# Byte margins for matmul operands, and an attention buffer that is shared with the scores

## The chip, the cores and the metric

The kernel runs on one core of a Trainium2 chip. The metric is the device time of one execution in microseconds (us), lower is better. The core has five engines that run their own instruction streams in order and wait for each other through semaphores: TensorE (PE, its weight loads listed apart as PEld), VectorE (DVE), ScalarE (ACT), GpSimd (POOL) and SyncE (SP, which here issues DMAs).

## The reference

One layer of an encoder over 512 tokens of width 1024. A combined projection of 11,328 columns feeds three branches: neighbourhood attention (16 heads of 64, a window of 8 by 16 on a grid 64 wide), a bidirectional Mamba-2 state-space mixer (8 groups, 32 heads), and two sigmoid gates that merge them. An output projection, two layer norms and a squared-ReLU feed-forward part (1024 to 4096 to 1024) follow.

```python
def hybrid_mixer(u, ...):
    proj = u @ w_in
    q, k, v, z, xbc, dt_raw, gate = jnp.split(proj, offs, axis=-1)
    ya = neighbourhood_attention(q, k, v, rpb) @ w_attn_br
    ...
    y = y * jax.nn.silu(z)            # y: the state-space scan, both directions
    ...
    ys = y @ w_ssd_br
    gates = jax.nn.sigmoid(gate + b_gate)
    merged = gates[:, :, 0] * ya + gates[:, :, 1] * ys
    return merged @ w_o

h = layer_norm(x, ln0_g, ln0_b)
h = layer_norm(ALPHA * h + hybrid_mixer(h, ...), ln1_g, ln1_b)
h = layer_norm(ALPHA * h + jnp.square(jax.nn.relu(h @ w1)) @ w2, ln2_g, ln2_b)
```

Within attention, for each head: scores are the scaled products of a query with the keys of its window plus a bias, softmax over the window, and the sum of values with these weights.

## The kernel before

All products are made in three: each fp32 operand is split into a high part and a low remainder (names ending in h and l, or wh and wl for weights), and `mm3` (lines 352 to 354) adds high times high, high times low and low times high in one PSUM bank. ScalarE makes the high part of a weight slab by a copy, and VectorE or GpSimd the low one by a subtraction. Slabs of weights have 8 blocks of 128 rows by 256 columns, 8 KB in each partition. Their high and low parts sit in two buffers each, of a pool named wp (tags wh and wl), which are reused through the whole kernel.

The stages, in order of time: first layer norm and transposes; eight groups of the state-space mixer, each with its projections (ps_x, and ps_z with the weights as the moving operand, 256 columns a product) beside the scan; attention; the attention branch's projection (ps_abr); the output projection (ps_o, 256 columns a product); the feed-forward part, whose first half product begins early in 256 columns; and the second feed-forward matrix, where the squared activations sq are the moving operand (ps_f from wh_f and sq). The mixer's order is made by a planner from costs; attention is written in plain order, and the framework's scheduler sets the order on each engine.

An operand of a product begins at some byte of its partition's memory. Which byte it is within 256 follows from the sizes of all tiles that stand ahead of it in the pools. Small unused tiles (rx_pad, ge_pad) set it here and there. As the tiles are laid out, in (moving operand, stationary operand): most 512-column products stand at (0, 0), those of wh_f with sq at (0, 128), z at (0, 0), group 0's x and the early feed-forward products at (0, 0), the output projection at (0, 96) and (192, 96), attention's scoring at (0, 64 or 128; 0), and the product of weights and values (po) at (128, 0).

Attention runs over 8 pairs of heads. For each head:

- TensorE makes two score banks pss (lines 1213 and 1214). VectorE adds the bias, writes the scores to sc and their maximum to mx (line 1218, a custom operation), and negates mx (1222).
- ScalarE takes the exponentials of the four quarters of sc in place and adds up sums (1224). VectorE inverts sums (reciprocal, 1226) and normalises sc (1228).
- TensorE transposes sc into two banks tp_p (1239). ScalarE copies each into pth (1243); VectorE subtracts for ptl (1244).
- TensorE makes po in ten products (1251 and 1252). Since the values' high and low parts stand side by side in the stationary operand vhl, one half of po's partitions holds the low part's sum. ScalarE copies it to low (1262), and VectorE adds both halves into aT (five additions, 1265).

sc has two buffers, so head h + 2 uses that of head h; low has a buffer of its own. Gate projections (ps_g, their sigmoid at line 1060) and the weights of later pairs are laid between heads by the scheduler. ScalarE loads a function table when it goes from the sigmoid to the exponential or back.

Of the kernel before, what the change touches and what calls it, by code (L numbers as in the profile page):

```python
# [11 lines left out]
F32 = mybir.dt.float32  # L12
F32R = mybir.dt.float32r
# [6 lines left out]
P = 128  # L20
# [3 lines left out]
KD = D // P  # L24
D_INNER = 2048
D_FF = 4096
NH = 16
HD = 64
# [5 lines left out]
OFF_Q, OFF_K, OFF_V, OFF_Z = 0, 1024, 2048, 3072  # L34
# [34 lines left out]
W0_ENG = lambda nc: (nc.gpsimd, nc.vector, nc.gpsimd, nc.vector)  # L69
# [3 lines left out]
class Plan:  # L73
# [16 lines left out]
                self.ap = self.make()  # L90
            return self.ap

    def tile(self, name, tag, pool, shape, dtype):
        return Plan.Tile(self, name, tag, lambda: pool.tile(shape, dtype, tag=tag, bufs=self.tags[tag],
                                                            name=name))

    def have(self, name, tag, ap):
        t = Plan.Tile(self, name, tag, None)
# [214 lines left out]
def encoder_layer(ctx, tc, x, w_in, w_attn_br, w_ssd_br, w_o, w_ff1, w_ff2, pcols, rows64,  # L313
                  d_skip, ln_rows, rpb_pad, consts, lmask, out, dbg=None):
    nc = tc.nc
# [6 lines left out]
    wp = ctx.enter_context(tc.tile_pool(name="wp", bufs=2))  # L322
# [20 lines left out]
                              op=ALU.subtract)  # L343
        return hi, lo

    def weights(parts, nk, ncol, name, eng=nc.vector, pool=None, after=None):
        hi = (pool or wp).tile([P, nk, ncol], F32R, tag="wh", name=f"wh_{name}")
        lo = (pool or wp).tile([P, nk, ncol], F32R, tag="wl", name=f"wl_{name}")
        return split_weights(parts, nk, ncol, name, hi, lo, eng, pool, after)

    def mm3(o, lh, ll, rh, rl, start, stop):
# [52 lines left out]
    gep = ge.__enter__()  # L404
# [33 lines left out]
    def by_dir(t, c, g):  # L438
# [13 lines left out]
    def local(name, tag, shape, dtype=F32):  # L452
        return plan.tile(name, tag, sbp, shape, dtype)

    def slab(name, parts, nk, ncol, engs):

        ws = plan.tile(f"ws_{name}", "ws", wp, [P, nk, ncol], F32)
        wh = plan.tile(f"wh_{name}", "wh", wp, [P, nk, ncol], F32R)
        wl = plan.tile(f"wl_{name}", "wl", wp, [P, nk, ncol], F32R)
        c = 0  # L460
        keys = []
        for j, (src, r0, c0, n) in enumerate(parts):
            op("SP", 4.0 * n / ncol, lambda src=src, r0=r0, c0=c0, n=n, c=c: nc.sync.dma_start(
                ws()[:, :, c : c + n],
                src[r0 : r0 + nk * P, c0 : c0 + n].rearrange("(k p) c -> p k c", p=P)),
               r=[("behind", 0)], w=[(ws.name, j)], at=4.8 if name == "x0" else 4.4)
            keys.append((ws.name, j))
            c += n
        hk = nk // 2
        for i, (k, eng) in enumerate(zip((slice(0, hk), slice(hk, nk)), engs)):  # L470
            op("ACT", 1.06, lambda k=k: nc.scalar.activation(wh()[:, k], ws()[:, k], AF.Copy),  # L471
               r=keys, w=[(wh.name, i)])
# [13 lines left out]
    def load_x(t):  # L486
# [7 lines left out]
       r=[(xts[0].name, 0)], w=[(xts[2].name, 0), ("behind", 0)])  # L494
# [11 lines left out]
    for t in range(NT):  # L506
        for j in range(2):
            op("DVE", 0.68, lambda t=t, j=j: v_.bn_stats(sts[t][:, j, :], xts[t]()[:, halves2[j]]),
               r=[(xts[t].name, 0)], w=[("st", t, j)])
        op("DVE", 0.2, lambda t=t: v_.bn_aggr(mv[:, t, :], sts[t]), r=[("st", t, 0), ("st", t, 1)],  # L510
           w=[("mv", t)])
    for ts in ((0,), (1,), (2, 3)):

        pr = slice(ts[0], ts[-1] + 1)
        vh, nv, y = lv[:, pr, 0], lv[:, pr, 1], rs[:, pr, 0]
        op("ACT", 0.28, lambda pr=pr, vh=vh: a_.activation(vh, mv[:, pr, 1], AF.Sqrt, bias=eps),
           r=[("mv", t) for t in ts], w=[("vh", ts[0])], table="sqrt")
# [12 lines left out]
    for t in range(NT):  # L530
# [19 lines left out]
       r=[(ws_dt.name, 0), (wh_dt.name, 0)], w=[(wl_dt.name, 0)], lock=True)  # L550
# [212 lines left out]

    def group_slabs(g):
        wb = slab(f"bc{g}", [(w_in, 0, OFF_B + g * P, P), (w_in, 0, OFF_C + g * P, P)], KD, 256,
                  (nc.gpsimd, nc.gpsimd) if g else W0_ENG(nc)[:2])
        wx = slab(f"x{g}", [(w_in, 0, OFF_X + g * 256, 256)], KD, 256,
                  (nc.gpsimd, nc.gpsimd) if g else W0_ENG(nc)[2:])
        return wb, wx

    def z_project(g):
        wh, wl = slab(f"z{g}", [(w_in, 0, OFF_Z + g * 256, 256)], KD, 256, (nc.gpsimd, nc.gpsimd))
        sz = local(f"sz{g}", "sz", [P, NT, 256])
        for c2 in range(2):
            ps = bank(f"ps_z{g}_{c2}", "mm", [P, 2, 256])
            for j in range(2):
                c = slice((2 * c2 + j) * P, (2 * c2 + j + 1) * P)
                for k in range(0, KD, 2):
                    def mms(k=k, j=j, c=c, ps=ps):
                        for q in (k, k + 1):  # L780
# [325 lines left out]
    vpool = tc.tile_pool(name="vp", bufs=1, reuse_waits="tile")  # L1106
    vpp = vpool.__enter__()

    vhl = vpp.tile([P, 4, NH // 2, 4, HD], F32R, name="vhl")

    hb = tc.tile_pool(name="hb", bufs=1, reuse_waits="tile")
    hbp = hb.__enter__()
# [43 lines left out]
    for pr in range(NH // 2):  # L1156
# [3 lines left out]

        qf = atp.tile([P, S], F32, tag="qf", name=f"qf{pr}")
        nc.scalar.activation(qf, psq, AF.Copy, scale=0.125)
        qs = atp.tile([P, 2, 4, 8, 16], F32R, tag="qs", name=f"qs{pr}")
        halves = (slice(0, HD), slice(HD, P))
        for hh, hp in enumerate(halves):
            for sv, dv in q_views(qf[hp], qs[hp, hh]):
# [15 lines left out]
        for hh in range(2):  # L1182
# [19 lines left out]
                    in1=cst[:, CC_M0 + half * P : CC_M0 + (half + 1) * P].rearrange(  # L1202
                        "p (r j) -> p r j", r=8), op=ALU.add)
            sc = atp.tile([P, 4, 256], F32, tag="sc", bufs=2, name=f"sc{h}")
            mx = atp.tile([P, 4], F32, tag="mx", bufs=2, name=f"mx{h}")
            sums = atp.tile([P, 4], F32, tag="sums", bufs=2, name=f"sums{h}")
            for m2 in range(2):
                pss = psx.tile([P, 2, 256], F32, tag="so", bufs=BANKS["so"], name=f"pss{h}_{m2}")
# [49 lines left out]
            pv(3, 0, 1, 3, False, False)  # L1258
            pv(3, 1, 1, 0, False, True)

            low = atp.tile([P, 4, P], F32, tag="low", name=f"low{h}")
            nc.scalar.activation(low[hp], po[HD - hh * HD : P - hh * HD], AF.Copy)
            pov, lov = (t[hp].rearrange("p m (r i) -> p m r i", r=8) for t in (po, low))
            for (dv, sv), (_, lv) in zip(q_views(aT[hp, pr, :], pov), q_views(aT[hp, pr, :], lov)):
# [30 lines left out]
    rx0 = tc.tile_pool(name="rx0", bufs=1, side="right", reuse_waits="tile")  # L1295
    rx0p = rx0.__enter__()
    rows0 = rx0p.tile([P, 2, D], F32, name="rows0")
    rx0p.tile([P, 8], F32, name="rx_pad")

    def first_norm(t, xt, eng):  # L1300

# [49 lines left out]
    w3p = ctx.enter_context(tc.tile_pool(name="w3", bufs=1, reuse_waits="tile"))  # L1351
    ep = tc.tile_pool(name="ep", bufs=1, reuse_waits="tile")
    epp = ep.__enter__()
    wo_pool = tc.tile_pool(name="wo", bufs=1, reuse_waits="tile")
    wop = wo_pool.__enter__()

# [16 lines left out]
    for t2 in range(2):  # L1373
        toks = (2 * t2, 2 * t2 + 1)
        for s in range(4):
            cs = slice(s * 256, (s + 1) * 256)
            wo = wos[s]
            tag = ("mm", "so")[s % 2]
            pss = {t: psx.tile([P, 256], F32, tag=tag, bufs=BANKS[tag], name=f"ps_o{t}_{s}")
                   for t in toks}  # L1380
            for k in range(KD):
                for t in toks:
                    ts_ = slice(t * P, (t + 1) * P)
                    mm3(pss[t], mgh[:, k, ts_], mgl[:, k, ts_], wo[0][:, k, :], wo[1][:, k, :],
                        k == 0, k == KD - 1)
            for t in toks:
                nc.vector.scalar_tensor_tensor(out=h0[t][:, cs], in0=h0[t][:, cs], scalar=ALPHA,
                                               in1=pss[t], op0=ALU.mult, op1=ALU.add)
        if t2:

            early = []
            for s in range(2):
                w1 = weights([(w_ff1, 0, s * 256, 256)], KD, 256, f"f1_0_{s}")
                for j in range(2):
                    tag = ("so", "yd", "cb", "so")[2 * s + j]
                    ps = psx.tile([P, S], F32, tag=tag, bufs=BANKS[tag], name=f"ps_f1_0_{2 * s + j}")
                    ff1_half(w1, j, ps, 0)
# [9 lines left out]

    ffp = ctx.enter_context(tc.tile_pool(name="ffp", bufs=1, reuse_waits="tile"))
    NQ = D_FF // D
    gep.tile([P, 24], F32, name="ge_pad")  # L1410
    pairs = [[gep.tile([P, 4, 256], F32R, tag="gt", bufs=4, name=f"sq{n}_{i}") for n in "hl"]
             for i in range(2)]
    turn = {"parts": 2, "raw": 0}
# [1 line left out]
    def parts(name, shape):  # L1415

        turn["parts"] += 1
        if turn["parts"] % 3 == 0:
            return third(w3p, name, shape)
        return [wp.tile(shape, F32R, tag=n, name=f"{n}_{name}") for n in ("wh", "wl")]  # L1420

    def raw(name):
        turn["raw"] += 1
# [273 lines left out]
```

## Time and profile before

| | before |
|---|---|
| median of 3 runs | 1207.59 us (1206.69 to 1209.53) |
| profiled execution | 1207.45 us, span 1205.7 us |
| instructions | 16822 |
| mean granted clock of TensorE | 0.995 |
| TensorE idle, 580 to 682.2 us | 1.46 us |
| VectorE idle, 580 to 682.2 us | 10.46 us |

The span is the time from the first to the last instruction of the profiled execution; 1.75 us of its time lie around it. In rows of groups, the columns are line, engine, operation, result and operands, shape, count, total busy us, mean ns of one, and the engine's idle time before these instructions with what ended it. In the timeline they are start and duration in us, then the same names.

### The profile page before, as it was taken

Reading aid. Unit: us, or ns where it says so; the run is one execution under the profiler, and the core shown is the slowest. Engines: PE = TensorE matmul, PEld = TensorE weight load, DVE = VectorE, ACT = ScalarE, POOL = GpSimd, SP = SyncE. Lnnn points to the kernel's source line nnn. Section 1 sums busy time; section 2 is a strip of 40 time slices with the busy share of each in tenths; the row PEclk is TensorE's granted clock in tenths of the full one; section 3 lists DMA queues with packets and bytes.
Section 4 is the critical chain, followed back from the end, with each engine's and each line's share of the span. In section 5 each row is a group of like instructions: output and inputs, shape, how many; then the busy total and the mean of one; then the engine's idle time right before and its main releaser. Section 6 shows DMA issues by size and latency. Waiting matters only on the chain.

```text
span 1205.7 us, 16822 instructions
## 1 busy us (share of the span) xinstructions
PE 1172.6 (97%) x6306; PEld 1004.4 (83%) x6306; DVE 780.4 (65%) x1427; ACT 608.9 (51%) x1012; POOL 541.9 (45%) x588
## 2 busy tenths in 40 slices
PE   5999999999999999999999989999999999999996
PEld 5988898989888888788888878889988888878885
DVE  7758475666666665434788975356772566398856
ACT  4576573836355563324667882342254454365410
POOL 1158977777788767303666730015153131221000
PEclk9999999999999999999999989999999999999998
DMA  7144243333333341233423323344238886778511
GB/s 231 54 144 140 88 140 105 107 117 128 105 105 112 117 138 70 71 105 89 110 60 81 84 101 109 105 145 134 72 105 207 214 202 180 189 205 216 162 49 52
DMA packets 131169, 149.21 MB, mean 124 GB/s; under 512 B 22928, under 2 KB 105488, under 8 KB 131088
## 3 DMA queue, kind: packets, MB, share of 16 engines
q1 hardware_dynamic: 118032, 113.54, 30.4%
q0 software_dynamic: 13056, 34.61, 11.8%
q8 instruction: 49, 0.80, 0.3%
q14 instruction: 32, 0.26, 0.1%
HBM read 145.90 MB, written 2.23 MB: 123 GB/s over the span
## 4 chain that ended last, share of the span: by engine, by line
PE 85%; DVE 5%; ACT 3%; DMA 3%; issue 3%; POOL 1%; SPq 0%; DVEq 0%; POOLq 0%; ACTq 0%
PE ps_f L354 8%; PE ps_f L353 8%; PE ps_f L352 8%; PE ps_x L354 5%; PE ps_x L352 5%; PE ps_x L353 5%; PE ps_z L352 3%; PE ps_z L353 3%; PE ps_z L354 3%; PE yd L932 2%; DMA w2r<-in_w_ff 2%; PE ps_sbr L352 2%; PE ps_sbr L354 2%; PE ps_sbr L353 2%; PE ps_g L352 2%
## 5 line engine op out<-in xcount | busy, mean ns | idle before, releaser
L741 DVE SCALAR_TENSOR_TENSOR cv<-ps_x,pc,cv 128x511 f32<-128x511 f32 (+1 forms) x128 | 95.8, 748 | 26.9 <-ACT cv L733 23.3
L353 PE MATMUL ps_f<-h1Th,wl_f 128*128 128x512 f32 (+1 forms) x288 | 104.7, 366 | 0.0
L352 PE MATMUL ps_f<-h1Th,wh_f 128*128 128x512 f32 (+1 forms) x288 | 104.3, 366 | 0.0
L354 PE MATMUL ps_f<-h1Tl,wh_f 128*128 128x512 f32 (+1 forms) x288 | 103.3, 367 | 1.1 <-DVE h1Tl L429 1.1
L1468 DVE TENSOR_TENSOR wl_f<-w2r,wh_f 128x1024 fp32r<-128x1024 f32 x42 | 49.8, 1220 | 64.2 <-ACT wh_f L1467 64.2
L352 PE MATMUL ps_z<-wh_z,hTh 128*128 128x256 f32 x256 | 75.9, 296 | 0.0
L354 PE MATMUL ps_z<-wl_z,hTh 128*128 128x256 f32 x256 | 72.4, 283 | 0.0
L353 PE MATMUL ps_z<-wh_z,hTl 128*128 128x256 f32 x256 | 72.3, 283 | 0.0
L1462 POOL DMA_DIRECT2D w2r<-in_w_ff x30 | 36.3, 1416 | 70.2 <-DMA w2r<-in_w_ff 46.2
L352 PE MATMUL ps_f<-wh_f,sqh 128*128 128x512 f32 x168 | 66.0, 396 | 0.7 <-ACT sqh L1467 0.7
L353 PE MATMUL ps_f<-wh_f,sql 128*128 128x512 f32 x168 | 66.2, 395 | 0.2 <-DVE sql L1468 0.2
L354 PE MATMUL ps_f<-wl_f,sqh 128*128 128x512 f32 x168 | 66.1, 395 | 0.0
L1048 DVE TENSOR_TENSOR ysacc<-ps_sbr,ysacc 128x512 f32<-128x512 f32 x56 | 38.5, 689 | 40.5 <-PE ps_sbr L354 40.3
L342 DVE TENSOR_TENSOR wl_f<-ws_f,wh_f 128x1024 fp32r<-128x1024 f32 x36 | 46.7, 1333 | 24.2 <-ACT wh_f L341 24.1
L353 PEld LDWEIGHTS ps_f<-h1Th,wl_f 128*128 128x128 f32 x288 | 54.2, 188 | 8.9
L354 PEld LDWEIGHTS ps_f<-h1Tl,wh_f 128*128 128x128 f32 x288 | 53.3, 188 | 10.0 <-DVE h1Tl L429 1.3
L352 PEld LDWEIGHTS ps_f<-h1Th,wh_f 128*128 128x128 f32 x288 | 54.1, 188 | 8.9
L1321 POOL TENSOR_TENSOR gt<-gt,ysacc 128x512 f32<-128x512 f32 x8 | 12.8, 1601 | 107.2 <-ACT gt L1060 99.1
L1467 ACT ACTIVATE wh_f<-w2r 128x1024 fp32r<-128x1024 f32 x42 | 42.5, 1052 | 34.4 <-DMA w2r<-in_w_ff 22.0
L352 PE MATMUL ps_x<-hTh,wh_bc 128*128 128x512 f32 (+1 forms) x144 | 56.9, 395 | 1.6 <-ACT wh_bc L471 1.6
L1451 POOL DMA_DIRECT2D w2r<-in_w_ff x18 | 16.1, 896 | 92.3 <-DVE wl_f L1468 55.8
L352 PE MATMUL ps_sbr<-yTh,wh_sbr 128*128 128x512 f32 x128 | 55.6, 434 | 1.2 <-DVE ysacc L1048 0.6
(327 smaller groups left out, 3900.2 us busy)
## 6 DMA issues: line engine op xcount, KB each, us to landing
ws_f<-in_w_ff SPq DMA_DIRECT2D x20, 1024.0 KB
w2r<-in_w_ff POOLq DMA_DIRECT2D x18, 1024.0 KB, 7.3
bc<-acs_d SPq DMA_DIRECT2D x32, 512.0 KB
w2r<-in_w_ff POOLq DMA_DIRECT2D x30, 512.0 KB, 8.6
ws_bc<-in_w_in SPq DMA_DIRECT2D x16, 512.0 KB
ws_x<-in_w_in SPq DMA_DIRECT2D x8, 1024.0 KB
ws_z<-in_w_in SPq DMA_DIRECT2D x8, 1024.0 KB
ws_g<-in_w_in SPq DMA_DIRECT2D x8, 1024.0 KB
```

Of the source, the lines that this page charges most:

```text
L342: (eng[i] if isinstance(eng, tuple) else eng).tensor_tensor(out=lo[:, k], in0=st[:, k], in1=hi[:, k].bitcast(F32), op=ALU.subtract)
L352: nc.tensor.matmul(o, lh, rh, start=start, stop=False)
L353: nc.tensor.matmul(o, ll, rh, start=False, stop=False)
L354: nc.tensor.matmul(o, lh, rl, start=False, stop=stop)
L741: op("DVE", 0.75, lambda j=j, o=o, n=n: nc.vector.scalar_tensor_tensor(out=acc()[:, o], in0=ps()[:, n], scalar=tap(j), in1=acc()[:, o], op ...
L932: nc.tensor.matmul(yd()[:, c % 2, h * HD : (h + 1) * HD], bc()[:, 1, h, :], xtok()[:, c, h * HD : (h + 1) * HD], start=True, stop=True)
L1048: op("DVE", 0.69, lambda d=d, ps=ps: nc.vector.tensor_tensor(out=ysacc[:, d, :], in0=ps(), in1=ysacc[:, d, :], op=ALU.add), r=[(ps.name, 0 ...
L1321: nc.gpsimd.tensor_tensor(out=g1, in0=g1, in1=ysacc[:, d, :], op=ALU.mult)
L1451: load = nc.gpsimd.dma_start(t, rows(i, n, c))
L1462: nc.gpsimd.dma_start(t, rows(i, n, c, k), accum_op=ALU.add)
L1467: nc.scalar.activation(hi[:, k], x, AF.Copy)
L1468: nc.vector.tensor_tensor(out=lo[:, k], in0=x, in1=hi[:, k].bitcast(F32), op=ALU.subtract)
```

## The change

It does two things. First, margins: slabs from the pool wp get 2112 columns instead of 2048, and a view that begins either 0 or 16 fp32 values (64 bytes) in; values (vhl) and scaled queries (qs) get such a margin of 64 bytes too, mx is made wider, and three unused tiles (rx_pad, ep_pad, ge_pad) change size. After it all 512-column products, those of wh_f with sq included, begin at byte 0 within 256 in both operands, and the 256-column ones stand at 0 and 64: z at (64, 0), the others with the stationary operand 64 on. Second, `low` is no longer a tile: it is the first half of the same head's sc.

```diff
+    def wide(t, nk, shift=0):
+        return t[:, shift : shift + 2048].rearrange("p (k c) -> p k c", k=nk)
-    def weights(parts, nk, ncol, name, eng=nc.vector, pool=None, after=None):
-        hi = (pool or wp).tile([P, nk, ncol], F32R, tag="wh", name=f"wh_{name}")
-        lo = (pool or wp).tile([P, nk, ncol], F32R, tag="wl", name=f"wl_{name}")
+    def weights(parts, nk, ncol, name, eng=nc.vector, pool=None, after=None, shift=0):
+        if pool:
+            hi, lo = [pool.tile([P, nk, ncol], F32R, tag=n, name=f"{n}_{name}") for n in ("wh", "wl")]
+        else:
+            hi, lo = [wide(wp.tile([P, 2112], F32R, tag=n, name=f"{n}_{name}"), nk, shift)
+                      for n in ("wh", "wl")]
...
-        wh, wl = slab(f"z{g}", [(w_in, 0, OFF_Z + g * 256, 256)], KD, 256, (nc.gpsimd, nc.gpsimd))
+        wh, wl = slab(f"z{g}", [(w_in, 0, OFF_Z + g * 256, 256)], KD, 256, (nc.gpsimd, nc.gpsimd), 16)
...
-    vhl = vpp.tile([P, 4, NH // 2, 4, HD], F32R, name="vhl")
+    vhl = vpp.tile([P, 8256], F32R, name="vhl")[:, 16:8208].rearrange(
+        "p (b r i q) -> p b r i q", b=4, r=NH // 2, i=4)
...
-        qs = atp.tile([P, 2, 4, 8, 16], F32R, tag="qs", name=f"qs{pr}")
+        qs = atp.tile([P, 1088], F32R, tag="qs", name=f"qs{pr}")[:, 16:1040].rearrange(
+            "p (h m r i) -> p h m r i", h=2, m=4, r=8)
...
-            mx = atp.tile([P, 4], F32, tag="mx", bufs=2, name=f"mx{h}")
+            mx = atp.tile([P, 24], F32, tag="mx", bufs=2, name=f"mx{h}")[:, :4]
...
-            low = atp.tile([P, 4, P], F32, tag="low", name=f"low{h}")
+            low = sc[:, 0:2, :].rearrange("p a (b i) -> p (a b) i", b=2)
...
-    rx0p.tile([P, 8], F32, name="rx_pad")
+    rx0p.tile([P, 48], F32, name="rx_pad")
...
+    epp.tile([P, 16], F32, name="ep_pad")
...
-                w1 = weights([(w_ff1, 0, s * 256, 256)], KD, 256, f"f1_0_{s}")
+                w1 = weights([(w_ff1, 0, s * 256, 256)], KD, 256, f"f1_0_{s}", shift=16)
...
-    gep.tile([P, 24], F32, name="ge_pad")
+    gep.tile([P, 56], F32, name="ge_pad")
```

The slabs of group 0 (`group_slabs`) and the buffers of the second feed-forward matrix (`parts`) are changed alike.

Only attention is put in another order; ahead of it and behind it each engine's instructions stand as before. On VectorE, around head 8 of the 16 (numbers at names: head, then the half or bank, then the buffer), there stood before:

```order
L1222 TENSOR_SCALAR mx8_6056<-mx8_6056 128x4
L342 TENSOR_TENSOR wl_qk7_6686<-ws_qk7_6687,wh_qk7_6685 128x1024 x2
L1226 RECIPROCAL sums8_6057<-sums8_6057 128x4
L1228 TENSOR_SCALAR sc8_6055<-sc8_6055,sums8_6057 128x256 x4
L1244 TENSOR_TENSOR ptl7_0_5920<-tp_p7_0_5914,pth7_0_5919 128x512
L1218 ISA sc9_6132,mx9_6133<-pss9_0_6135,bias9_6127 128x256
...
L1265 TENSOR_TENSOR aT_4690<-po6_5855,low6_5866 64x8x16 x3
```

The split of a later pair's weights stood between the negated maximum and the reciprocal, and the scoring of head 9 began ahead of head 6's additions. In the changed kernel, for heads 7 and 8:

```order
L1233 TENSOR_SCALAR mx7_5881<-mx7_5881 128x4
L1237 RECIPROCAL sums7_5882<-sums7_5882 128x4
L1239 TENSOR_SCALAR sc7_5880<-sc7_5880,sums7_5882 128x256 x4
L1276 TENSOR_TENSOR aT_4690<-po6_5849,sc6_5804 64x8x16 x3
L1276 TENSOR_TENSOR aT_4690<-po6_5849,sc6_5804 64x8x8 x2
L1229 ISA sc8_6047,mx8_6048<-pss8_0_6050,bias8_6042 128x256
...
L1233 TENSOR_SCALAR mx8_6048<-mx8_6048 128x4
L1237 RECIPROCAL sums8_6049<-sums8_6049 128x4
L1239 TENSOR_SCALAR sc8_6047<-sc8_6047,sums8_6049 128x256 x4
```

The scoring of head 8 stands behind the additions of head 6, and the reciprocal directly behind the negated maximum.

On ScalarE, at the end of attention, before:

```order
L1224 ACTIVATE sc15_6867,sums15_6869<-sc15_6867,mx15_6868 128x256 x4
L1243 ACTIVATE pth14_0_6822<-tp_p14_0_6817 128x512
L1262 ACTIVATE low13_6678<-po13_6667 64x512
L1243 ACTIVATE pth14_1_6831<-tp_p14_1_6826 128x512
L1060 ACT_TABLE_LOAD
L1060 ACTIVATE gt1_1_6999<-ps_g3_1_7026,pc_82 128x512
L1243 ACTIVATE pth15_0_6899<-tp_p15_0_6894 128x512
L1262 ACTIVATE low14_6846<-po14_6835 64x512
L1243 ACTIVATE pth15_1_6908<-tp_p15_1_6903 128x512
L1262 ACTIVATE low15_6923<-po15_6912 64x512
```

And in the changed kernel:

```order
L1069 ACT_TABLE_LOAD
L1069 ACTIVATE gt1_1_6983<-ps_g3_1_7010,pc_82 128x512
L1273 ACTIVATE sc13_6609<-po13_6654 64x512
L1254 ACTIVATE pth14_0_6808<-tp_p14_0_6803 128x512
L1254 ACTIVATE pth14_1_6817<-tp_p14_1_6812 128x512
L1273 ACTIVATE sc14_6776<-po14_6821 64x512
L1235 ACT_TABLE_LOAD
L1235 ACTIVATE sc15_6852,sums15_6854<-sc15_6852,mx15_6853 128x256 x4
L1254 ACTIVATE pth15_0_6884<-tp_p15_0_6879 128x512
L1254 ACTIVATE pth15_1_6893<-tp_p15_1_6888 128x512
L1273 ACTIVATE sc15_6852<-po15_6897 64x512
```

The last head's exponentials, which came before the copies of heads 13 and 14, now come behind both, and behind another table load. On TensorE the last pair's products move accordingly: of the gate projections, 36 products stood behind the last product of po12 before, and 12 do now; the scoring of head 14 (eight products) and four transposes of head 13 stood ahead of it and now stand behind.

More of the change, by code (lines that the diff above doesn't have):

```diff
@@ L91, in __call__, with tile @@
             return self.ap
-    def tile(self, name, tag, pool, shape, dtype):
-        return Plan.Tile(self, name, tag, lambda: pool.tile(shape, dtype, tag=tag, bufs=self.tags[tag],
-                                                            name=name))
+    def tile(self, name, tag, pool, shape, dtype, view=lambda t: t):
+        return Plan.Tile(self, name, tag, lambda: view(pool.tile(
+            shape, dtype, tag=tag, bufs=self.tags[tag], name=name)))
     def have(self, name, tag, ap):
@@ L453, in local, with slab @@
         return plan.tile(name, tag, sbp, shape, dtype)
-    def slab(name, parts, nk, ncol, engs):
+    def slab(name, parts, nk, ncol, engs, shift=0):
         ws = plan.tile(f"ws_{name}", "ws", wp, [P, nk, ncol], F32)
-        wh = plan.tile(f"wh_{name}", "wh", wp, [P, nk, ncol], F32R)
-        wl = plan.tile(f"wl_{name}", "wl", wp, [P, nk, ncol], F32R)
+        wh, wl = [plan.tile(f"{n}_{name}", n, wp, [P, 2112], F32R, lambda t: wide(t, nk, shift))
+                  for n in ("wh", "wl")]
         c = 0
@@ L765, in group_slabs @@
         wb = slab(f"bc{g}", [(w_in, 0, OFF_B + g * P, P), (w_in, 0, OFF_C + g * P, P)], KD, 256,
-                  (nc.gpsimd, nc.gpsimd) if g else W0_ENG(nc)[:2])
+                  (nc.gpsimd, nc.gpsimd) if g else W0_ENG(nc)[:2],
+                  0 if g else 16)
         wx = slab(f"x{g}", [(w_in, 0, OFF_X + g * 256, 256)], KD, 256,
-                  (nc.gpsimd, nc.gpsimd) if g else W0_ENG(nc)[2:])
+                  (nc.gpsimd, nc.gpsimd) if g else W0_ENG(nc)[2:],
+                  0 if g else 16)
         return wb, wx
     def z_project(g):
-        wh, wl = slab(f"z{g}", [(w_in, 0, OFF_Z + g * 256, 256)], KD, 256, (nc.gpsimd, nc.gpsimd))
+        wh, wl = slab(f"z{g}", [(w_in, 0, OFF_Z + g * 256, 256)], KD, 256, (nc.gpsimd, nc.gpsimd), 16)
         sz = local(f"sz{g}", "sz", [P, NT, 256])
@@ L1419, in parts @@
             return third(w3p, name, shape)
-        return [wp.tile(shape, F32R, tag=n, name=f"{n}_{name}") for n in ("wh", "wl")]
+        return [wide(wp.tile([P, 2112], F32R, tag=n, name=f"{n}_{name}"), shape[1])
+                for n in ("wh", "wl")]
     def raw(name):
```

## The prediction

> **What bounds the kernel now.** I read the page's busy times first, then the chain that ended last by engine, then the windows, by stage.
>
> ```profile
> PE 1172.6 (97%) x6306; PEld 1004.4 (83%) x6306; DVE 780.4 (65%) x1427; ACT 608.9 (51%) x1012; POOL 541.9 (45%) x588
> PE 85%; DVE 5%; ACT 3%; DMA 3%; issue 3%; POOL 1%; SPq 0%; DVEq 0%; POOLq 0%; ACTq 0%
> ```
>
> TensorE is busy 97% of the span and is 85% of the chain. So two things can move the time: how fast products follow each other, and new gaps of TensorE. Columns below: stretch, its length, busy us (instructions) of PE, PEld, DVE, ACT, POOL, then granted clock, DMA share, GB/s.
>
> ```profile
> 60.00:550.00 490.00, 486.87 (x2689) 417.45 (x2688) 297.04 (x486) 266.44 (x394) 337.25 (x348) 1.00 0.35 112
> 580.00:612.80 32.80, 31.99 (x174) 26.99 (x173) 29.05 (x71) 20.73 (x61) 23.69 (x39) 1.00 0.31 76
> 612.80:647.90 35.10, 34.70 (x208) 30.24 (x207) 31.42 (x97) 25.48 (x73) 23.45 (x40) 1.00 0.33 76
> 647.90:682.20 34.30, 34.05 (x202) 29.58 (x201) 31.27 (x96) 24.87 (x73) 23.38 (x41) 1.00 0.33 78
> 682.20:718.10 35.90, 32.63 (x190) 27.88 (x190) 25.85 (x90) 31.09 (x65) 17.97 (x25) 0.95 0.21 65
> ```
>
> In the projections (60 to 550) VectorE is busy 61% of the time and TensorE 99%. In the middle of attention (580 to 682.2) TensorE is still at 98.5%, but VectorE at 91.74 of 102.2 us: both are nearly full, and only 10.5 us of VectorE are free. That stage has no room for a wait on VectorE; the projections have plenty.
>
> **The change, part 1: margins.** They change where operands begin within 256 bytes. For the 512-column products of the second feed-forward matrix (ps_f from wh_f, wl_f and sq) the pair goes from 0 and 128 to 0 and 0; the other 512-column products stand at 0 and 0 already. The same tile with both orders of operands is in the trace (last columns: total busy us, mean ns):
>
> ```profile
> L352 PE MATMUL ps_f<-wh_f,sqh 128*128 128x512 f32 x168 | 66.0, 396 | 0.7 <-ACT sqh L1467 0.7
> L353 PE MATMUL ps_f<-wh_f,sql 128*128 128x512 f32 x168 | 66.2, 395 | 0.2 <-DVE sql L1468 0.2
> L354 PE MATMUL ps_f<-wl_f,sqh 128*128 128x512 f32 x168 | 66.1, 395 | 0.0
> L352 PE MATMUL ps_f<-h1Th,wh_f 128*128 128x512 f32 x224 | 87.1, 389 | 0.0
> L353 PE MATMUL ps_f<-h1Th,wl_f 128*128 128x512 f32 x224 | 87.2, 389 | 0.0
> L354 PE MATMUL ps_f<-h1Tl,wh_f 128*128 128x512 f32 x224 | 87.1, 390 | 0.0
> ```
>
> Misaligned products take 396, 395 and 395 ns, aligned ones 389, 389 and 390: 18 ns for each of 168 triples, a gain of 3.0 us. These run one behind the other on TensorE, so all of it counts; the bounds are 0 (the 6 ns come from something else) and 3.0.
>
> 256-column products are put 64 bytes apart: 768 of z, 192 of group 0's x, 192 early feed-forward ones (all from 0 apart), and 384 of the output projection (from 96 apart). No row shows 64. Nearest rows, weight loads (means):
>
> ```profile
> L353 PEld LDWEIGHTS ps_z<-wh_z,hTl 128*128 128x128 f32 x256 | 48.9, 191 | 1.1 <-issue 0.7
> L352 PEld LDWEIGHTS ps_o<-wh_o,mgh 128*128 128x128 f32 x128 | 24.0, 188 | 0.0
> L1252 PEld LDWEIGHTS po<-ptl,vhl 128*128 128x128 f32 x80 | 15.6, 195 | 1.1 <-DVE ptl L1244 0.2
> L1239 PEld LDWEIGHTS tp_p<-cst,sc 128*128 128x128 f32 x128 | 14.7, 140 | 2.2 <-DVE sc L1228 0.5 <-DVE ptl L1244 0.5
> ```
>
> At 0 apart a load takes 191 ns, at 96 apart 188, at 128 apart (po) 195. I take the row nearest to 64, that of 96, and its difference for the step between products: 3 ns for each of 768 + 192 + 192 = 1152 products, 3.5 us, and nothing for the output projection, which is near 96 already. Bounds: a loss of 4 ns (195 against 191) on 1152 and of 7 ns (195 against 188) on 384, together 7.3 us; on the gain's side, the transposes' 140 ns would come to 59 us at face value, but a load lies beside the product before it, and products cannot follow each other faster than their columns go:
>
> ```profile
> 698.65 0.28 PE L1213 MATMUL pss<-kh,qs 128*128 128x256 f32 x1
> 699.50 0.28 PE L1214 MATMUL pss<-klz,qs 128*128 128x256 f32 x1
> 699.85 0.40 PE L354 MATMUL ps_g<-hTl,wh_g 128*128 128x512 f32 x1
> 703.03 0.39 PE L353 MATMUL ps_g<-hTh,wl_g 128*128 128x512 f32 x1
> ```
>
> The first two are the first and the last of eight scoring products: 0.85 us in seven steps, 121 ns each. The others are 14 steps apart, 227 ns each for 512 columns, so 114 for 256. A gain is then at most 7 to 8 ns for each of 1536 products, 12 us. The 288 products of attention (pss, po) are also shifted, but that stage is taken as a whole in part 2. The paddings themselves add no instruction. Sum of part 1: −6.5 us.
>
> [...]
>
> **Part 2: the shared buffer.** low becomes the first half of sc. As sc has two buffers, the scoring of head h+2 (VectorE's custom operation, L1218) now waits until the additions into aT of head h have read low. Before, it runs ahead:
>
> ```profile
> 632.67 0.40 DVE L1218 CUSTOM_DVE_ANT_0 sc<-pss,bias 128x256 f32<-128x256 f32 x1
> 641.14 0.99 DVE L1265 TENSOR_TENSOR aT<-po,low 64x128 f32<-64x128 f32 x5
> L1226 DVE RECIPROCAL sums<-sums 128x4 f32<-128x4 f32 x16 | 2.8, 173 | 8.1 <-ACT sc L1224 7.8
> ```
>
> The first is head 7's scoring, the second head 5's additions 8.5 us later: that order is forbidden now. In the changed order (shown above for two heads) the reciprocal stands directly behind the negated maximum, with nothing between, for heads 0, 4, 6, 7, 8, 9, 11 and 13; before, for 0 and 15 alone. VectorE then waits out ScalarE's whole exponential. Before, all 16 reciprocals together waited only 8.1 us, since weight splits and ptl work of another head stood between. Behind the waiting reciprocal stand that head's normalising, then aT, ptl and the next scoring, and so TensorE's transposes and po. What one such wait costs comes from the tail, where ScalarE runs undisturbed:
>
> ```profile
> 697.85 0.27 PE L1252 MATMUL po<-ptl,vhl 128*128 128x128 f32 x1
> 698.58 0.51 ACT L1224 ACTIVATE sc<-sc,mx 128x256 f32<-128x256 f32 x1
> 700.47 0.19 ACT L1224 ACTIVATION_READ_ACCUMULATOR sc<-sc,mx 128x1 f32 x1
> 700.90 1.81 DVE L1228 TENSOR_SCALAR sc<-sc,sums 128x256 f32<-128x256 f32 x4
> 702.63 0.93 DVE L1265 TENSOR_TENSOR aT<-po,low 64x128 f32<-64x128 f32 x5
> 703.49 0.67 DVE L1244 TENSOR_TENSOR ptl<-tp_p,pth 128x512 fp32r<-128x512 f32 x1
> 704.09 0.40 DVE L1218 CUSTOM_DVE_ANT_0 sc<-pss,bias 128x256 f32<-128x256 f32 x1
> 705.46 0.07 DVE L1218 DVE_READ_ACCUMULATOR2_ANT mx<- 128x1 f32 x1
> 706.43 0.62 PE L1239 MATMUL tp_p<-cst,sc 128*128 128x128 f32 x4
> 709.59 1.28 ACT L1060 ACT_TABLE_LOAD   x1
> 710.89 0.69 ACT L1060 ACTIVATE gt<-ps_g,pc 128x512 f32<-128x512 f32 x1
> 712.75 0.59 ACT L1262 ACTIVATE low<-po 64x512 f32<-64x512 f32 x1 [0.69 <-ACT pth L1243]
> 713.36 0.60 ACT L1243 ACTIVATE pth<-tp_p 128x512 fp32r<-128x512 f32 x1
> 718.10 0.79 PE L352 MATMUL ps_abr<-aTh,wh_abr 128*128 128x512 f32 x1 [1.38 <-ACT aTh L1276]
> ```
>
> The four exponentials last from 698.58 to 700.66, 2.08 us, about 2.1 with the hand-over. **Middle:** six more heads (4, 6, 7, 8, 9, 11) make 12.6 us of waiting on an engine with 10.5 us free. If VectorE's old idle could all be traded, +2.1 remains; if none of it, +12.6, and more where scoring itself is late for the next head (up to +17, two more waits). The old idle was itself waiting for other engines (of the 8.1 us ahead of reciprocals 7.8 for ScalarE), so little of it can be traded; I take +11.
>
> **Tail:** t = 0 is the end of head 12's last product, 698.12 before; ps_abr starts at 718.10, 20.0 later. Now scoring and exponentials of heads 14 and 15 come one after the other. ScalarE's order puts exp13 at −1.8 to 0.25, behind a gate's sigmoid (0.69) and a table (1.28). VectorE: normalising 13 to 2.2, aT12 (0.93) to 3.2, scoring 14 (704.09 to 705.53, 1.44) and negation to 4.85. ScalarE: three of exp14 to 6.4, pth13 (0.6), the last exp, pth13 (0.6) to 8.1, table and sigmoid to 10.1; VectorE meanwhile ptl13 (0.67 each) and normalising 14 to 10.1; po13's last products to 10.35, low13 (0.59) 11.0, aT13 12.0. Only now, behind two ptl14, may 15 be scored: 12.0 + 1.3 + 1.4 = 14.7. ScalarE: low14 15.0, table 16.3, exp15 18.4. Then normalising (0.2 + 1.81) 20.2, transposes 20.7, pth and ptl 22.4, po15 23.2, and low, aT and aTh as before (about 1.4) 24.6. That is 4.6 later than 20.0, and 24 gate products of TensorE stand ahead of t = 0 now that stood behind it, less eight of scoring and four transposes: 24 × 0.227 − 12 × 0.12 = 4.0 us. Together +8.6. A further term is the clock:
>
> ```profile
> 715.00:720.00 5.00, 3.62 (x13) 3.04 (x13) 2.54 (x8) 3.17 (x6) 0.00 (x0) 0.50 0.30 109
> ```
>
> Sparse work at the tail's end already brings 0.50. With longer gaps I add 0.06 us (half of 0.12) on some 24 short products of heads 14 and 15, 1.5 us. Tail +10, bounds +6 and +13 (two units of hand-over, or the table kept).
>
> **Sum.** The profiled execution took 1207.45 (span 1205.7 and 1.75 around it; the median of the runs is 1207.59): 1207.45 + 11 + 10 − 6.5 = 1222.0.
>
> **Rivals.**
> - **A, other side: VectorE's idle absorbs the waits.** From 580 to 718.1 it has 10.5 + 10.05 = 20.5 us of it, and TensorE has independent gate products to fill with. Then the stage stays and the margins remain: 1207.45 − 6.5 = 1201. It decides where the stage's growth stays under 4 us. For it: TensorE is still at 98.5% there. Against: 91.74 + 12.6 us on VectorE exceed 102.2.
> - **B, margins do nothing** (the change doesn't do what it says): 1207.45 + 21 = 1228.5. For it: 6 ns are also within what different tiles differ by. Against: three groups of three agree to 1 ns.
> - **C, only the tail lengthens**, the middle hiding its waits behind TensorE: 1207.45 + 10 − 6.5 = 1211.
>
> **How the numbers follow.** Forecast 0.72, A 0.08, B 0.10, C 0.10. The forecast's bounds (middle 2 to 17, tail 6 to 13, margins −15 to +7) rarely meet at their ends; 1210 to 1233 holds most of it, and includes B and C. Down to 1208 the range also takes in the weaker end of C; A lies outside. This kernel can tell about 0.2%, 2.4 us, from no change: faster, under 1205.2, is A, 0.08; between 1205.2 and 1210.0 lie the edges of A and C, 0.06; slower has 0.86.
>
> **What would show it.** Part 1: the three groups of wh_f with sq at 389 ns, z's weight loads at 188, and the stretch from 60 to 550 some 2 to 4 us shorter. Part 2: idle ahead of the reciprocal from 8.1 to about 20 us, ps_abr's first product at about 718 + 21 less the gain before attention, and a longer stretch at a clock under 1.00 behind it. Wrong would be: a ps_abr that comes under 4 us later than 718.1 (the gain before it taken out), or a z whose loads get slower at 64 apart.

## The result, and the profile after

| | before | changed |
|---|---|---|
| median | 1208.45 us (1206.69 to 1212.47, 6 runs) | 1236.22 us (1233.39 to 1239.51, 6 runs) |
| ratio, 95% interval | | 1.0229 (1.0206 to 1.0252) |
| profiled execution's span | 1205.7 us | 1233.6 us |
| first product of ps_q | 552.6 us | 550.4 us |
| first product of ps_abr | 718.1 us | 748.8 us |
| from there to the end | 487.6 us | 484.8 us |

The change costs 2.3%. The direction was forecast; the size was not: 1236 lies above the range's end of 1233. The last three lines place it. In the profiled executions attention lost 32.9 us, and the kernel gained 2.2 us ahead of it and 2.8 behind. Those two gains are small against the spread: in the later profiles of kernels with the same instructions ahead of attention, ps_q began between 550.4 and 553.5 us, and from ps_abr to the end the same instructions took 481.1 to 486.9.

The changed kernel's busy times on its page:

```profile
PE 1181.0 (96%) x6306; PEld 1010.6 (82%) x6306; DVE 775.9 (63%) x1427; ACT 609.0 (49%) x1012; POOL 542.8 (44%) x588
```

TensorE is busy 8.4 us longer over the whole span, with the same instructions. Its windows (length; busy us of PE, PEld, DVE, ACT, POOL; granted clock, DMA share, GB/s) show attention as a whole, and the four pieces in which the clock was low (the last runs on into ps_abr):

```profile
550.40:748.80 198.40, 175.72 (x898) 147.83 (x896) 129.29 (x386) 117.24 (x306) 102.41 (x165) 0.90 0.27 64
624.50:632.00 7.50, 5.77 (x19) 4.91 (x20) 6.73 (x20) 3.86 (x11) 5.48 (x9) 0.54 0.49 144
662.00:669.50 7.50, 5.37 (x23) 4.59 (x23) 7.38 (x13) 4.96 (x15) 6.73 (x8) 0.54 0.10 18
689.50:696.50 7.00, 5.79 (x14) 4.55 (x15) 3.95 (x16) 3.27 (x10) 3.50 (x7) 0.51 0.50 155
730.50:754.50 24.00, 16.85 (x57) 13.32 (x57) 14.78 (x45) 14.92 (x28) 1.27 (x1) 0.50 0.17 56
```

Attention before, and its one such piece:

```profile
552.60:718.10 165.50, 160.78 (x897) 137.72 (x896) 132.54 (x386) 117.84 (x307) 101.54 (x165) 0.99 0.32 78
714.50:722.00 7.50, 6.12 (x20) 4.98 (x21) 4.95 (x12) 5.17 (x10) 0.00 (x0) 0.54 0.48 186
```

Two readings. TensorE's idle time in attention went from 165.50 − 160.78 = 4.7 us to 198.40 − 175.72 = 22.7, so 18.0 us of the 32.9 are waits. The other 14.9 us (175.72 − 160.78) are *busy* time of the same products: they got slower. Before, the clock was at about half in one stretch of 7.5 us; now in four, of 46 us together. (Both sums are pieced together from half-us windows.) The two widest waits, and the one ahead of ps_abr, on TensorE's timeline:

```profile
690.71 0.80 PE L359 MATMUL ps_g<-hTh,wh_g 128*128 128x512 f32 x1 [5.31 <-ACT qf L1172]
...
742.29 1.94 PE L1250 MATMUL tp_p<-cst,sc 128*128 128x128 f32 x8 [4.76 <-DVE sc L1239]
748.79 0.80 PE L359 MATMUL ps_abr<-aTh,wh_abr 128*128 128x512 f32 x1 [1.33 <-ACT aTh L1287]
```

In the first row a 512-column product takes 0.80 us where 0.39 is usual: the granted clock was 0.50 in the window from 690.5 to 691 us. The groups that the prediction named, by form (last columns: busy us, mean ns, idle ahead of them):

```profile
L359 PE MATMUL ps_f<-wh_f,sqh 128*128 128x512 f32 x168 | 65.1, 390 | 1.2 <-ACT sqh L1480 1.2
L360 PEld LDWEIGHTS ps_z<-wh_z,hTl 128*128 128x128 f32 x256 | 48.2, 188 | 1.1 <-issue 0.7
L1276 DVE TENSOR_TENSOR aT<-po,sc 64x128 f32<-64x128 f32 x48 | 11.1, 282 | 19.5 <-ACT sc L1273 19.4
L1237 DVE RECIPROCAL sums<-sums 128x4 f32<-128x4 f32 x16 | 2.8, 175 | 23.8 <-ACT sc L1235 23.8
```

The squares' products went from 396 to 390 ns, z's weight loads from 191 to 188. VectorE's idle ahead of the reciprocals went from 8.1 to 23.8 us, and ahead of the additions into aT from 4.3 to 19.5. Its timeline shows the new order at work:

```profile
653.50 0.18 DVE L1237 RECIPROCAL sums<-sums 128x4 f32<-128x4 f32 x1 [2.21 <-ACT sc L1235]
654.77 0.93 DVE L1276 TENSOR_TENSOR aT<-po,sc 64x128 f32<-64x128 f32 x5
655.87 0.42 DVE L1229 CUSTOM_DVE_ANT_0 sc<-pss,bias 128x256 f32<-128x256 f32 x1 [0.17 <-DVE aT L1276]
```

The additions of head 6 end, and 0.2 us later head 8 is scored. In all 14 such pairs scoring follows the additions, by 0.1 to 2.3 us.

### The profile page after: what moved, and what is told of

The parts are those of the page before. It is cut to its first block, busy times and chain, and to the rows that moved or that the text cites. A ratio compares the mean times of both kernels' runs of the same rounds, so it can differ in the third digit from the quotient of the medians.

```text
span 1233.6 us, 16816 instructions
## 1 busy us (share of the span) xinstructions
PE 1181.0 (96%) x6306; PEld 1010.6 (82%) x6306; DVE 775.9 (63%) x1427; ACT 609.0 (49%) x1012; POOL 542.8 (44%) x588
## 5 line engine op out<-in xcount | busy, mean ns | idle before, releaser
L1475 POOL DMA_DIRECT2D w2r<-in_w_ff x30 | 36.3, 1416 | 74.2 <-DMA w2r<-in_w_ff 48.9
L342 DVE TENSOR_TENSOR wl_f<-ws_f,wh_f 128x1024 fp32r<-128x1024 f32 x36 | 46.7, 1333 | 21.7 <-ACT wh_f L341 21.4
L359 PE MATMUL ps_g<-hTh,wh_g 128*128 128x512 f32 x128 | 51.9, 405 | 5.3 <-ACT qf L1172 5.3
```

The source lines that it names most:

```text
L342: (eng[i] if isinstance(eng, tuple) else eng).tensor_tensor(out=lo[:, k], in0=st[:, k], in1=hi[:, k].bitcast(F32), op=ALU.subtract)
L359: nc.tensor.matmul(o, lh, rh, start=start, stop=False)
L1475: nc.gpsimd.dma_start(t, rows(i, n, c, k), accum_op=ALU.add)
```

## The experiments

Three theories stood open. *Sharing*: the loss is all from the shared buffer, and the margins gain. *Margins hurt*: values and queries 64 bytes on slow attention down. And within the first: is it the waits alone, or also the clock that falls after them?

**Each half alone.** In the first kernel low lies in the same head's second pth buffer, dead by then, and is written in its type, fp32r; every engine's order is that of before. The second is the kernel before with low shared, in the changed kernel's order.

```diff
-            low = sc[:, 0:2, :].rearrange("p a (b i) -> p (a b) i", b=2)
+            low = pts[1][0].rearrange("p a b i -> p (a b) i")
```

> The changed kernel with all its margins, but low lies in the head's own second pth buffer (written in fp32r) instead of in sc; every engine's instructions stand in the order of before. Theory 'sharing' (the whole loss comes from scoring that waits for the additions, the margins alone gain what their rows show: 2.7 us in the squares' products, 2.2 us ahead of attention): ps_abr's first product at about 716 instead of 748.8, time 1208.4 - 5 = about 1203.5, ratio 0.996. Rival 'margins hurt attention' (values and queries 64 bytes on make attention's products slower): about 1236, attention still some 30 us longer. Rival 'margins do nothing in total': 1208.

> The kernel before with nothing changed but low as the first half of sc: no margins, and every engine's order that of the changed kernel. Theory 'sharing': attention as long as in the changed kernel, 33 us over before, time 1208.4 + 33 = about 1241, ratio 1.027; the same four stretches of a clock at or under 0.6. Rival 'margins hurt attention': about 1208.

Measured: 1200.82 us, ratio 0.9938 (0.9923 to 0.9954), and 1242.72 us, ratio 1.0282 (1.0265 to 1.0298). Attention in the first, then in the second:

```profile
551.30:716.10 164.80, 160.08 (x898) 136.92 (x896) 132.69 (x386) 117.89 (x307) 101.53 (x165) 1.00 0.32 78
```

```profile
553.30:751.90 198.60, 175.09 (x898) 147.24 (x897) 129.36 (x386) 117.14 (x306) 102.67 (x165) 0.91 0.26 64
```

So the two halves are separate: the margins gain about 7 us (1207.71 to 1200.82), the sharing costs about 35 (to 1242.72). Together that is 28 us, as the whole change costs (1208.45 to 1236.22). "Margins hurt" falls, and so does rival B of the prediction. The first kernel is faster than both.

**Which byte distance.** As that first kernel, with the 16-value shifts set to 0, 32 (128 bytes) or 24 (96 bytes).

```diff
-... (nc.gpsimd, nc.gpsimd), 16)       # and every other shift of 16
+... (nc.gpsimd, nc.gpsimd), 0)        # 32 and 24 in the other two
```

> As the first kernel of this call, but all 64-byte shifts are 0: z, group 0's x, the early feed-forward halves, queries and values begin at byte 0 within 256 again, and only the squares' products (and the widths of the tiles) differ from before. Theory 'byte distance counts for both kinds': 2.7 us of gain remain, the 2.2 us ahead of attention go: about 1205.7; z's weight loads at 191 ns. Rival 'the 512-column products alone gain': as the first kernel, 1203.5. [...]

> As the first kernel of this call, but the shifts are 128 bytes. Theory 'any distance but 0 serves': z's weight loads at 188 ns, about 1203.5. Rival '128 is as bad as the rows of po (195 ns) and of the squares (395 ns) made it look': z's loads at 191 to 195 ns, 2 to 5 us over the first kernel.

> As the first kernel (margins, low in pth), but the shifts of the 256-column operands are 96 bytes instead of 64. If the output projection's row in before (188 ns at 96 apart) holds for all: z's weight loads at 188 ns and about 1201. Rival 'only 64 serves': z's loads at 189 to 191 ns and about 1205.

Measured: 1205.40 us, ratio 0.9976 (0.9963 to 0.9989); 1205.06, 0.9974 (0.9963 to 0.9986); 1204.56, 0.9976 (0.9962 to 0.9990). Aligning the squares' products is worth about 3 us, putting the 256-column operands that were at 0 apart at 64 bytes another 4 to 5 (to the first kernel's 1200.82); 96 and 128 gave none of it. z in the kernel before, in the first kernel (64), and in the kernel at 96 (products, then loads):

```profile
L352 PE MATMUL ps_z<-wh_z,hTh 128*128 128x256 f32 x256 | 75.9, 296 | 0.0
...
L359 PE MATMUL ps_z<-wh_z,hTh 128*128 128x256 f32 x256 | 75.1, 293 | 0.6 <-DVE cv L748 0.6
...
L359 PE MATMUL ps_z<-wh_z,hTh 128*128 128x256 f32 x256 | 75.7, 296 | 0.3 <-DVE cv L748 0.3
L360 PEld LDWEIGHTS ps_z<-wh_z,hTl 128*128 128x128 f32 x256 | 48.2, 188 | 1.1 <-issue 0.7
```

Its loads take 188 ns as at 64 apart, but its products are at 296 as before; at 64 they were at 293. The load's duration, which the forecast used as the price, wasn't the price. Only its size happened to agree. Nor is 96 slow everywhere: the output projection stood at 96 apart before and at 64 in the changed kernel, and kept its pace:

```profile
L352 PE MATMUL ps_o<-wh_o,mgh 128*128 128x256 f32 x128 | 35.7, 282 | 0.0
...
L359 PE MATMUL ps_o<-wh_o,mgh 128*128 128x256 f32 x128 | 35.8, 282 | 0.0
```

In z, x and the early feed-forward products, all these kernels shift one operand and leave the other at 0. So they don't tell whether the distance counts or the byte at which one operand begins.

**The clock.** The changed kernel, every engine held to its order, with idle products that read hTh and write a bank nobody reads, put just ahead of the products that waited; first as many as fill the waits, then half.

```diff
+    idle = psx.tile([P, S], F32, tag="cb", bufs=BANKS["cb"], name="ps_idle")
+    fill = [nc.tensor.matmul(idle[:, :512], hTh[:, 0, :P], hTh[:, 0, :512], start=True, stop=True).ins
+            for _ in range(93)]                       # 50 in the second
...
+            tc.add_manual_dep(q, p.name, nosync, reason="order")   # q behind p, on every engine
```

> The changed kernel in its own order on every engine, with 93 idle products (512 columns, into a bank that nothing reads) put ahead of the twelve products for which TensorE waited 0.3 to 5.3 us in attention, as many as fill each wait at 0.227 us. They add work and take no wait of another engine away. Theory 'clock' (some 13 of attention's 33 us are products run at a lowered clock after gaps): no stretch under 0.9 in attention, TensorE's real products as fast as before, time about 1223 to 1227, some 10 to 13 us under the changed kernel's 1236. Rival 'waits alone' (the lowered clock lies beside other engines' chains and costs nothing): 1236 or more, even with the clock at 1.00. Rival 'the clock falls for another reason than idle products': the same four low stretches, 1236 or more.

> As the kernel above with half as many idle products (50) at the same twelve places, so that each wait is left half as long. Theory 'clock, by the length of what is idle': the stretches behind the gaps of 5.3 and 4.8 us (2.6 and 2.4 left) still fall, the others don't; time between, about 1229 to 1232. Rival 'any interruption counts': as the changed kernel, 1236. Rival 'a little work is enough': as the kernel above.

Measured: 1225.40 us, ratio 1.0146 (1.0117 to 1.0175), and 1230.05, ratio 1.0171 (1.0134 to 1.0207). Adding 93 useless products made the kernel 10 to 11 us faster (10.8 by the medians, 10.0 by the ratios). Attention with all waits filled; then with half, its whole and two neighbouring pieces:

```profile
550.60:741.60 191.00, 186.34 (x991) 154.47 (x989) 130.15 (x386) 117.14 (x306) 102.64 (x165) 1.00 0.27 67
```

```profile
552.10:748.60 196.50, 183.25 (x948) 151.62 (x946) 130.01 (x386) 117.17 (x306) 102.47 (x165) 0.96 0.26 65
686.00:691.00 5.00, 2.54 (x12) 1.76 (x10) 4.91 (x6) 2.69 (x5) 4.85 (x6) 1.00 0.02 3
691.00:698.00 7.00, 6.21 (x15) 4.94 (x16) 4.69 (x20) 3.27 (x10) 3.08 (x6) 0.51 0.51 157
```

With the waits filled the clock is 1.00, attention is 7.4 us shorter, and the part behind it another 3.4 (ps_abr no longer begins at half clock: 1.00 in all half-us windows from 540 to 770 us, where the changed kernel had 0.50 up to 754). Half filled, three stretches at 0.50 remain instead of four (from 629.5, 691 and 742 us on), one of them behind a wait that still lasted 3.2 us: the last row but one is that wait, the last what followed. So the expectation was right about the two widest waits, and the clock also fell at one narrower wait (TensorE idle for 1.2 us between 626.5 and 628.5, and for 0.7 between 623.5 and 625). The half-filled kernel's time can't be told from its neighbours' on either side, since the intervals overlap; what it shows are these stretches.

**The order.** low in pth again, so that no scoring has to wait for it, but every engine held to the changed kernel's order.

```diff
+            tc.add_manual_dep(q, p.name, nosync, reason="order")   # the changed kernel's order
-            low = sc[:, 0:2, :].rearrange("p a (b i) -> p (a b) i", b=2)
+            low = pts[1][0].rearrange("p a b i -> p (a b) i")
```

> low lies in the head's own pth buffer, so no scoring has to wait for it, but every engine is held to the changed kernel's order. Theory 'order' (the shared buffer costs through the order that it forces on VectorE, in which the reciprocal waits out the exponential): as the changed kernel, 1234 to 1238, idle ahead of the reciprocal about 24 us. Rival 'wait' (scoring is held up at run time by the buffer): about 1201 to 1215.

Measured: 1235.58 us, ratio 1.0227 (1.0199 to 1.0256), the changed kernel's own. So the order alone is enough for the whole loss; no wait for the buffer at run time is needed. Of this order, the shared buffer forces only that the scoring of head h + 2 stands behind the additions of head h. How much of the loss comes from that, and how much from what else the scheduler chose, this kernel doesn't separate.

**What in that order.** Two more kernels keep the shared buffer and the order but for a few instructions. One moves three pairs of weight splits on VectorE to between negation and reciprocal; the other moves products of attention on TensorE ahead of projections.

```diff
 VectorE, heads 7, 9 and 11
-wl split, wl split, ... scoring, negated maximum, reciprocal
+scoring, negated maximum, wl split, wl split, reciprocal
 TensorE
-ps_k (heads 10 and 11) ..., po5, tp_p6, ..., po6        ps_g2 ..., po10, pss12, ... tp_p11, ... po11
+po5, tp_p6, ps_k ..., po6, ...                          po10, ps_g2 ..., pss12, tp_p11, ... po11
```

> The changed kernel, every engine held to its order, but on VectorE three pairs of weight splits (wl_qk7, and wl_g of the last two gate slabs; 2.6, 3.0 and 2.8 us) are moved from ahead of the negated maximum of heads 7, 9 and 11 to between it and the reciprocal, as before had such work there. Theory 'the reciprocal waits out the exponential, 2.2 us a head, and VectorE's chain is what stretches attention': idle ahead of the reciprocals from 23.8 to about 17, attention 5 to 8 us shorter, more if one stretch of half clock goes: 1226 to 1231. Rival 'VectorE would have waited for low and pth anyway': the idle moves to the additions, 1234 to 1238.

> The changed kernel, every engine held to its order, but on TensorE some products of attention go ahead of projections that nobody waits for yet: po5 and the transposes of head 6 (by 3 to 6 us), po6, po10 (7 us), the scoring of head 12, the transposes of head 11 (6 us) and po11. VectorE's and ScalarE's orders stay, so each reciprocal stands where it did. Theory 'loop' (with the shared buffer head h + 2 is scored only after head h's additions, so two heads in flight turn over once per latency from scoring to additions, 22.3 us now and 17.8 before; what shortens that latency on any engine shortens the stage): attention 5 to 10 us shorter though the idle ahead of the reciprocals stays at 22 to 24; 1225 to 1231. Rival 'VectorE's waits at the reciprocals are the cost': as the changed kernel, 1234 to 1238.

Measured: 1233.61 us, ratio 1.0202 (1.0178 to 1.0225), and 1245.07, ratio 1.0308 (1.0286 to 1.0330). Both expectations of the first missed: the time can't be told from the changed kernel's, though attention in the profile is 3.0 us shorter (195.4). Its groups on VectorE:

```profile
L1278 DVE TENSOR_TENSOR aT<-po,sc 64x128 f32<-64x128 f32 x48 | 11.1, 283 | 21.4 <-ACT sc L1275 21.4
...
L1239 DVE RECIPROCAL sums<-sums 128x4 f32<-128x4 f32 x16 | 2.8, 172 | 17.2 <-ACT sc L1237 17.2
```

The idle ahead of the reciprocals went from 23.8 to 17.2, 6.6 us as meant, but 1.9 us of it came back ahead of the additions, and attention kept more than half. The second kernel failed both theories: it got slower by some 9 us, at the same 23.8 us ahead of the reciprocals. The timelines of ScalarE and TensorE show what happened at the first of these places:

```profile
646.50 0.60 ACT L1174 ACTIVATE qf<-ps_q 128x512 f32<-128x512 f32 x1 [4.37 <-POOL qs L1183]
647.13 0.59 ACT L1275 ACTIVATE sc<-po 64x512 f32<-64x512 f32 x1
647.74 1.09 ACT L1256 ACTIVATE pth<-tp_p 128x512 fp32r<-128x512 f32 x2
...
648.89 0.36 PE L1264 MATMUL po<-pth,vhl 128*128 128x256 f32 x1 [1.78 <-ACT pth L1256]
```

po5 was done at 641.8, but its copy to low stood on ScalarE behind qf, which waited 4.4 us for GpSimd's qs; pth6 stood behind that, and po6 on TensorE, moved up, waited 1.8 us for it and held up the projections that had been ahead of it. Moving one engine's instructions alone did not mend the order here; the later places were not followed one by one.

**The fast version's tail.** The first kernel, with 12 idle products ahead of attention's last three waits.

```diff
+    idle products: 2 ahead of po14, 5 ahead of po15, 5 ahead of ps_abr
```

> The kernel with margins and low in pth, in its own order, with 12 idle products ahead of the three last waits of attention (0.46, 1.29 and 1.33 us). Theory 'clock': the stretch at 0.66 behind attention goes to 1.00; about 2 us under 1200.8, so 1199. Rival: no change, or the idle products hold up ps_abr and it is 1201 to 1202.

Measured: 1199.13 us, ratio 0.9933 (0.9908 to 0.9958). The stretch's clock goes from 0.84 to 1.00 (without, then with the idle products), but its interval and the first kernel's overlap:

```profile
709.00:719.00 10.00, 6.88 (x35) 5.42 (x34) 7.16 (x22) 7.24 (x13) 1.28 (x1) 0.84 0.15 34
```

```profile
709.00:719.00 10.00, 9.71 (x50) 7.41 (x51) 7.19 (x19) 7.26 (x14) 1.28 (x1) 1.00 0.23 62
```

## Why the prediction was wrong

**The sum, term by term**, in the profiled executions:

| term | forecast | measured |
|---|---|---|
| margins | −6.5 us | −5.0 us in the profile of the changed kernel; about −7 alone |
| TensorE's waits, middle of attention | +11 | +11.0 (1.45 to 12.42 us, up to the end of po12) |
| TensorE's waits, tail | +8.6 | +7.0 (3.27 to 10.26 us) |
| attention's products slower by the clock | +1.5, in the tail only | +10.5 (busy 175.7 us; 165.2 with the waits filled) |
| attention's products slower for the rest | none | +4.4 (165.2 against 160.8 before) |

The 165.2 us are the filled kernel's 186.34 less 93 idle products of 0.227. The measured column adds up to +27.9, from 1207.45 to 1235.4. It must, since it only divides the difference of two profiled executions (1207.45 and 1235.38). The border between its last two lines is rough by some 2 us: counted from each product's start to the next, the filled kernel's own products take 162.8 us in place of 165.2.

**The failed step is the clock's term.** The prediction had the row with a clock of 0.50 at the end of attention before it, and priced it as 0.06 us on 24 short products, in the tail alone: 1.5 us, where the runs showed about 10.5. The new waits in the middle were counted, but not what they do to the products beside and behind them. At each of the three clusters of waits there (3.3 us around 621 to 626, 3.6 around 660 to 665, 5.3 at 685) the clock went to 0.50, for stretches of 7.5, 7.5 and 7 us, and at the tail's for 24. The filled kernel settles it: with the clock kept up, the kernel comes to 1225.4, next to the forecast 1222. The 10.5 us are busy time; of them attention gets back 7.4 in the filled kernel, since TensorE then waits longer for the other engines (25.8 us with the idle products counted as waits, against 22.7), and another 3.4 us come from the part behind attention. The range's upper end failed for the same reason: the pieces added to it in the middle and the tail (up to 17 and 13) bounded waits, with no term for the clock in the middle, and 1233 assumed that they rarely meet at their ends.

The last line of the table isn't settled. In the prediction's rows of before, products of 0.28 and 0.39 to 0.40 us begin 0.121 and 0.227 us apart, so each overlaps with the next. Where a wait stands behind a product, its whole length counts as busy time. By the author's estimate from these numbers that gives a term of this sign, but no run took it apart.

**The waits' sum was right, its reason only in part.** Six more heads whose exponential VectorE waits out, 12.6 us cut to 11, met the measured 11.0, in part by luck: taking 6.6 us of just those waits away gave 3.0 us of attention back, so the price a head was not 2.1. What fits the kernels with the shared buffer better is a loop: from the start of a head's scoring to the end of its additions, and from there to the scoring two heads on. Worked out from VectorE's rows (mean over heads 2 to 13, and over 14 pairs): before, a head took 26.4 us, and scoring began 8.0 us *ahead* of the additions; changed, it takes 21.8 and scoring begins 0.9 *behind* them. Two heads thus turn over in 22.7 us instead of 18.4; seven turns make 30 us, nearly the 32.9. The scheduler's new order did shorten the loop by 4.6 us, half of the 8.9 that the buffer took. In the kernel with the splits moved the loop's latency is 21.4, in that with products moved 23.2: seven turns that differ by −0.4 and +1.4 us make −2.8 and +9.8, where attention changed by −3.0 and +8.4. This is bookkeeping and no cause of its own; which queue sets the 21.8 us differs from head to head, and was not settled.

**The margins went as forecast** in size (−6.5 against about −7 alone); the squares' rows sum to 195.7 us from 198.3, 2.6 for the forecast's 3.0. "The row nearest to 64, that of 96" was a wrong reading: z, x and the early feed-forward products gained nothing in time at 96. One sign that was named for the margins was not seen: from the same product of z near 60 us to the first of ps_q it took 492.6 us before and 491.6 in the changed kernel, where 2 to 4 us were forecast, and the kernels with the same instructions there spread over 491.4 to 494.1.

**The rivals.** A (VectorE's idle absorbs the waits) and C (only the tail lengthens) fell with the waits in the middle. B fell with the first kernel. 64 bytes changed the pace of 256-column products: z's three rows went from 296, 283 and 283 ns before to 293, 279 and 279 in the first kernel. By what mechanism, no run shows.

## What to carry to other kernels

Before a buffer is shared, ask which engine's *order* it fixes: count how far the next user ran ahead of the last reader in the trace (8 us here), and how many rounds there are (7 here). That product, 56 us, is a rough upper estimate of the loss; 33 us of attention were lost. A buffer that was already dead within the same round cost nothing here (attention 164.8 us in the first kernel, 165.5 before). When a change opens waits on TensorE, price the clock behind them as well as the waits: here 18 us of waits brought 10 to 11 us more. Moving up one engine's instructions gained nothing here while the engines that it waits for kept their order (1245.07 us against the changed kernel's 1236.22).

## What the hardware showed

- The granted clock fell to 0.50 after waits well under 5 us: in the kernel before, after 0.46 and 1.33 us within 4 us (0.50 from 715 us on), in the half-filled kernel after 2.2 us in one piece (740 to 742 us). A single wait of 1.2 us (at 506 and at 876 us in the first kernel) left it at 1.00. Seen through half-us windows, the low stretches of all these kernels' attention last 3.5 to 4 or 7 to 7.5 us, or 14 to 24.5 where waits go on.
- Useless products can pay: 93 of them, 21 us of TensorE's time put into its waits, made a kernel 10 to 11 us faster (1225.40 us against 1236.22).
- The 256-column products of z, of group 0's x slab and of the early feed-forward half took 2 to 6 ns less with operands 64 bytes apart within 256 than at 0 (the changed kernel and the first against before; 283 to 279 ns for two of z's three rows), and at 96 and 128 at most 2 ns less; those of the output projection took the same within 1 ns at 96 and at 64 (281 to 284). The 512-column products of wh_f or wl_f with the squares took 5 to 6 ns less with both operands at 0 than at 0 and 128 (390 ns in the changed kernel and the first, 395 to 396 before; 392 to 394 in the kernel with the shifts at 0).
